# Eight of the 24 modulation groups computed between the prompt's attention maps, their weights loaded by Pool's queue

## The chip, the core and the metric

One core of one Trainium2 chip runs the whole program. The metric is the device time of one execution in microseconds (us). The kernel before took 1636.48 us (median of three runs). Engines are named as in the profile: PE (TensorE), DVE (VectorE), ACT (ScalarE), POOL (GpSimd) and SP (SyncE, which issues nearly all transfers; its queue of issues is SPq, Pool's is POOLq).

## The reference, cut to what matters

One layer of a streaming encoder, for a prompt of 512 rows and a running stream of 32 rows, width 1024, in float32:

```
mod = silu(c) @ w_ada + b_ada            -> shift1, scale1, gate1, shift2, scale2, gate2
h   = x * (1 + scale1) + shift1
z   = h @ w_in + b_in                    -> conv value, conv gate, q, k, v
conv: GLU -> causal depthwise conv (31 taps) -> LayerNorm -> swish
attention: rotary q/k, 4 heads, (softmax1 - lambda * softmax2) @ v, RMSNorm
x   = LN1(alpha * x + gate1 * (concat(conv, attn) @ w_out + b_out))
x   = LN2(alpha * x + gate2 * PEER(x * (1 + scale2) + shift2))
```

`w_ada` is 1024 by 6144, read once: 24 MB. Shift 1 and scale 1 are needed before anything else; gate 1 in the output projection; shift 2 and scale 2 after the first LayerNorm; gate 2 only at the very end.

## The kernel before, in words

The modulation is computed in 24 **groups** of 256 columns; group n belongs to vector n // 4 (shift 1, scale 1, gate 1, shift 2, scale 2, gate 2). `ada(n)` loads two tiles of 512 KB (r = 0 and 1), runs eight narrow float32 matmuls into a PSUM tile `pat` (L154), has ACT copy the result into `modrow` (L157), and queues the group in `PEND`. One group later `ada_end` closes it: for the four vectors in `cols` two tiny matmuls (L170) and a DVE write (L171); for groups from 8 on a load of the bias `bada` on SP (L176), a matmul with `sel4` (L178), a DVE add into `mrow` (L180) and a store to `mod_d` on SP (L181). PSUM tiles `sm` and `pat` come from two rings of two buffers each, which the attention uses too.

The stages, in program order:

1. Groups 0 to 7, the input x, and the first two column blocks of `w_in`.
2. Four channel blocks of the conv's value and gate (`zunit`, L194: one weight load, an ACT cast `wh` and a DVE rest `wl`, then 48 matmuls); after each block three groups, 8 to 19 in all. The GLU result goes to `U`; from then on the depthwise conv can run: 124 **taps** on DVE (L272, L275), one after the other on the accumulator `acc`, handed out by `conv(n)`.
3. The value columns (L322, L327, L333) in two halves, after each two groups, 20 to 23.
4. Keys and queries: `zqk(h)` for four heads. Each is two units of 48 matmuls (one for k, one for q), an ACT copy `z`, four transfers on SP that swap 32-row blocks into `zw` (L466), and three DVE operations (L468, L469, L471) which make the rotated `qk`; the key also goes out (L474).
5. Attention per head, four query blocks i: scores (L493), row maxima (L352), exponentials on ACT (L363), the difference map `a` (L383), transposes (L499), the product with v (L504), and `head_out`. Before head 2 come the rest of the taps and `conv_norm` (L401 to L418), before head 3 the sample's attention (L431 to L452).
6. The output projection (L607 to L631), LayerNorm, the PEER queries, and then the long pass over the two expert tables (to the end of the program).

What is written is not the order of execution: a scheduler orders each engine's instructions before the run, within the dependences and the rings. The taps are tied to each other by an order-only dependence. Transfers on SP leave in the order in which they stand in its queue, and an issue that waits holds back those behind it.

Weight tiles `wr` of all stages share a ring of eight buffers of 512 KB:

```
    def wload(src):
        t = wp.tile([128, D], F32, tag="wr", name="wr", bufs=WB)
        SY.dma_start(t, src)
        return t
```

Of the kernel before, what the change touches and what calls it, by code (L numbers as in the profile page):

```python
# [8 lines left out]
F32 = mybir.dt.float32  # L9
# [10 lines left out]
D = 1024  # L20
# [32 lines left out]
ROWB = 4  # L53
GSC = 2.0 ** 15
WB = 8
SLOT = 4.6
COST_U = 1.2
COST_V = 2.2
# [17 lines left out]
def build(tc, I, O):  # L76
# [3 lines left out]
    V, S, G, PE, SY = nc.vector, nc.scalar, nc.gpsimd, nc.tensor, nc.sync  # L80
# [12 lines left out]
    def pat():  # L93
        return pa.tile([128, 512], F32, tag="pa", name="pat")
# [24 lines left out]
    wp = pool(r1, "wp", 4, side="right")  # L119
# [13 lines left out]
# [4 lines that stand above are left out]
# [9 lines left out]
        V.tensor_sub(lo, t, hi.bitcast(F32))  # L146
        return hi, lo

    def ada(n, ps_=None):
        p = (ps_ or pat)()  # L150
        for r in range(2):
            w = wload(I["w_ada"][n, r])
            for g in range(4):
                PE.matmul(p[32 * g:32 * g + 32, :256], sil[:, r * 4 + g, :], w[:, g * 256:(g + 1) * 256],  # L154
                          start=(r == 0), stop=(r == 1), tile_position=(0, 32 * g))
        row = wp.tile([128, 256], F32, tag="modrow", name="modrow", bufs=3)
        S.copy(row, p[:, :256])  # L157
        PEND.append((n, row))
        if len(PEND) > 1:
            ada_end(*PEND.pop(0))  # L160

    PEND = []

    def ada_end(n, row):
        kind, q = divmod(n, 4)
        nm = ("sh1", "sc1", "g1", "sh2", "sc2", "g2")[kind]
        if nm in cols:
            c = sm()
            for s in range(2):
                PE.matmul(c[:, 2 * s:2 * s + 2], row[:, s * 128:(s + 1) * 128], sel4, start=True, stop=True)  # L170
            V.scalar_tensor_tensor(cols[nm][:, 2 * q:2 * q + 2, :], c[:, 0:4].rearrange("p (a b) -> p a b", b=2),  # L171
                                   float(nm[:2] == "sc"), bmod[nm][:, 2 * q:2 * q + 2, None].to_broadcast([128, 2, 2]),
                                   op0=OP.add, op1=OP.add)
        if kind >= 2:
            bt = wp.tile([2, 256], F32, tag="bada", name="bada", bufs=2)
            SY.dma_start(bt, bcast_rows(I["b_ada"][n * 256:(n + 1) * 256], 2))  # L176
            c = sm()
            PE.matmul(c[:2, :256], sel4, row, start=True, stop=True)  # L178
            rw = wp.tile([2, 256], F32, tag="mrow", name="mrow", bufs=1)
            V.tensor_add(rw, c[:2, :256], bt)  # L180
            SY.dma_start(mod_d[:, n * 256:(n + 1) * 256], rw)  # L181
# [47 lines left out]
    zp = pool(r5, "zp", 1, side="right")  # L229
# [18 lines left out]
    adas = iter(range(8, 24))  # L248
    for c in range(4):
        p1 = zbig(4 + c) if c else zfirst[0]  # L250
        sg = zp.tile([128, 2, HT], F32, tag="z", name="sg", bufs=2)
        S.activation(sg, p1[:, :, :HT], AF.Sigmoid, bias=bzc[:, 4 + c:5 + c])
        p0 = zbig(c) if c else zfirst[1]
        np2 = NP - HT
        for d0, h, s0, s1 in ((30, 0, 0, HT), (30 + HT, 1, 0, np2), (572, 1, np2, HT)):
            V.scalar_tensor_tensor(U[:, c, d0:d0 + s1 - s0], p0[:, h, s0:s1], bzc[:, c:c + 1], sg[:, h, s0:s1],
                                   op0=OP.add, op1=OP.mult)
        for n in range(3):
            ada(next(adas))
    SY.dma_start(O["convp"], U[:, :, 512:542])  # L260
    SY.dma_start(O["convs"], U[:, :, 574:604])
# [22 lines left out]
    def conv(n):  # L284
        for _ in range(n):
            next(taps, None)
# [25 lines left out]
    for n in range(2):  # L312
        wv = [wsplit(I["w_v"][n, kh]) for kh in range(2)]
        wf = WRAW[-2:]
        for i in range(NT):
            p = pat()
            r = ROWS[i]
            cs = [slice((k % 4) * 256, (k % 4 + 1) * 256) for k in range(KC)]
            if i < 4:
                for q, (a, b) in enumerate(((hh, 0), (hl, 0), (hh, 1))):  # L320
                    for k in range(KC):
                        PE.matmul(p[:, :256], a[:, k, i * 128:(i + 1) * 128], wv[k // 4][b][:, cs[k]],  # L322
                                  start=(q == 0 and k == 0), stop=(q == 2 and k == KC - 1))
            else:
                for k in range(KC):
                    o = k % 4 * 32
                    PE.matmul(p[o:o + 32, :256], hs[:, k, :], wf[k // 4][:, cs[k]], start=(k < 4), stop=(k >= 4),  # L327
                              tile_position=(0, o))
                vs4 = zp.tile([128, 256], F32, tag="vs4", name="vs4", bufs=1)
                S.copy(vs4, p[:, :256])  # L330
                p = sm()
                PE.matmul(p[:NS, :256], selrep[:, :NS], vs4, start=True, stop=True)
            V.tensor_add(vt[:r, i, n * 256:(n + 1) * 256], p[:r, :256], bv[:r, n * 256:(n + 1) * 256])  # L333
            if n == 1:
                SY.dma_start(O["v"][i * 128:i * 128 + r], vt[:r, i, :])
            conv(1)
        ada(next(adas))
        ada(next(adas))
    ada_end(*PEND.pop(0))
    S.activation(lsum, lsum, AF.Exp)  # L340
    V.tensor_sub(neglam, lsum[:, 1:2], lsum[:, 0:1])
    V.tensor_scalar(neglam, neglam, -LAM0, None, op0=OP.add)
# [137 lines left out]
    for h in range(4):  # L480
        if h < 3:
            qks.append(zqk(h + 1))
        qh, kh = qks[h]
        if h == 2:
            conv(124)
            conv_norm()
        if h == 3:
            sample_att()
        for i in ((0, 1, 2, 3) if h < 3 else (3, 0, 1, 2)):
            kl = 128 * (i + 1)  # L490
            sc = big()
            for m in range(2):
                PE.matmul(sc[:, m, :kl], qh[pT[m], i * 128:(i + 1) * 128], kh[pT[m], :kl], start=True, stop=True)  # L493
            V.memset(sc[:64, :, kl - 64:kl], NEG)
            e = at.tile([128, 2, 512], F32, tag="e", name="e")
            (a,), rs = softmax_parts([sc[:, :, :kl]], [e[:, :, :kl]], False)
            pt = sm()
            for kb in range(i + 1):
                PE.transpose(pt[:, kb * 128:(kb + 1) * 128], a[:, kb * 128:(kb + 1) * 128], ident)  # L499
            aT = at.tile([128, 512], F32, tag="aT", name="aT")  # L500
            (V.tensor_copy if h >= 3 else S.copy)(aT[:, :kl], pt[:, :kl])
            po = sm() if h < 3 else pat()
            for kb in range(i + 1):
                PE.matmul(po[:, :128], aT[:, kb * 128:(kb + 1) * 128], vt[:, kb, h * 128:(h + 1) * 128],  # L504
                          start=(kb == 0), stop=(kb == i))
            head_out(po[:, :128], i, h, 128, rs)
            conv(CB)
    r5.close()
    r4.close()
    l2 = ExitStack()  # L510
# [11 lines left out]
    for i in (4, 3, 0, 1, 2):  # L522
        r = ROWS[i]
# [574 lines left out]
    for q in range(2):  # L1098
        p = pat()
# [89 lines left out]
```

## Time and profile before

| what | before |
|---|---|
| three runs, us | 1636.06, 1636.48, 1637.83 |
| profiled execution, us | 1637.79 |
| its span, first to last instruction, us | 1635.8 |
| mean granted TensorE clock | 0.978 |
| PE busy | 1561.1 us (95%) |
| DVE busy | 1387.9 us (85%) |
| ACT busy | 611.2 us (37%) |
| POOL busy | 470.4 us (29%) |
| chain that ended last | PE 73%, DVE 13%, DMA 7% |

Busy time is the time in which an engine has an instruction under way; matmuls are pipelined, so a busy PE is not PE at its peak. The shares are averages over stages with different limits; stages 1 to 5 above fill the first 271 us, stage 6 the rest. A row of the timeline gives the start, the busy time, the engine, the line, output and inputs, the count, and in brackets the idle time ahead of it with what ended it.

### The profile page before, as it was taken

The page shows a single profiled execution, that of the slowest core. Times are in us where ns is not written, and L with a number is a line of the kernel's source. Part 1 is how long each engine was busy: PE and PEld are TensorE (multiplying, and loading weights), DVE is VectorE, ACT ScalarE, POOL GpSimd, SP SyncE. Part 2 cuts the span into 40 slices and gives each one's busy share as a digit, 9 for nine tenths or more (in the row PEclk, how much of TensorE's full clock was granted, in tenths as well). Part 3 has the DMA queues.
Part 4 walks back from the last instruction along what each step waited for, and adds up shares of the span by engine and source line. Part 5 has one row for each costly group of instructions (what it writes and reads, how often), then busy time and mean ns, then how long its engine had stood idle before and what let it go on. Part 6 is the DMA issues. An engine that isn't in the chain of part 4 may idle for free.

```text
span 1635.8 us, 24708 instructions
## 1 busy us (share of the span) xinstructions
PE 1561.1 (95%) x8887; PEld 1343.7 (82%) x8887; DVE 1387.9 (85%) x2680; ACT 611.2 (37%) x1059; POOL 470.4 (29%) x325
## 2 busy tenths in 40 slices
PE   7999987999989999999999899999999999999996
PEld 4777854786669999999999798888888888888884
DVE  3888988799999999999898568888778778788897
ACT  3312456342122444444454333333333333333332
POOL 0000000000144445247424123533334233244440
PEclk8999988999999999999999999999999999999998
DMA  9767333374478889999999999999999999999993
GB/s 348 282 193 258 87 117 122 97 225 141 157 242 283 293 279 314 342 351 337 365 350 376 354 311 313 345 358 342 349 338 342 340 329 352 337 321 329 336 327 104
DMA packets 184537, 465.58 MB, mean 285 GB/s; under 512 B 17536, under 2 KB 85184, under 8 KB 181216
## 3 DMA queue, kind: packets, MB, share of 16 engines
q1 hardware_dynamic: 138336, 296.23, 52.2%
q0 software_dynamic: 46080, 167.79, 29.1%
q8 instruction: 69, 1.13, 0.3%
q14 instruction: 52, 0.43, 0.1%
HBM read 415.57 MB, written 45.77 MB: 282 GB/s over the span
## 4 chain that ended last, share of the span: by engine, by line
PE 73%; DVE 13%; DMA 7%; issue 3%; ACT 2%; SPq 1%; DVEq 0%; POOL 0%; ACTq 0%; POOLq 0%
PE acc L1040 32%; PE pat L957 27%; PE big L194 3%; PE pat L731 2%; DMA rowg<-in_u_ji_dram,idx 2%; PE big L872 2%; PE big L620 1%; DVE jkg L904 1%; PE pat L154 1%; DVE acc L275 1%; DMA wr<-in_w_ada_dram 1%; DVE lo L948 1%; DVE s L710 1%; DMA wr<-in_w_in_dram 1%; DMA zw<-z 1%
## 5 line engine op out<-in xcount | busy, mean ns | idle before, releaser
L893 POOL DMA_INDIRECT rowg<-in_u_ji_dram,idx x160 | 210.9, 1318 | 790.5 <-DVE VT L707 438.4
L948 DVE TENSOR_TENSOR lo<-raw,hi 128x1024 fp32r<-128x1024 f32 x256 | 311.9, 1220 | 111.2 <-ACT hi L946 106.1
L946 ACT CAST hi<-raw 128x1024 fp32r<-128x1024 f32 x256 | 266.6, 1046 | 310.7 <-PE acc L1040 217.5
L893 POOL DMA_INDIRECT rowg<-in_vd_dram,idx x160 | 257.8, 1611 | 324.5 <-DVE accB L915 98.6
L1040 PE MATMUL acc<-hi,Pl 128*128 128x512 f32 x768 | 301.5, 393 | 0.0
L1040 PE MATMUL acc<-lo,Ph 128*128 128x512 f32 x768 | 281.4, 390 | 0.0
L1040 PE MATMUL acc<-hi,Ph 128*128 128x512 f32 x768 | 245.7, 394 | 3.7 <-issue 3.7
L957 PE MATMUL pat<-h2h,hi 128*128 128x384 f32 x1024 | 213.4, 343 | 5.9 <-ACT hi L946 2.8
L957 PE MATMUL pat<-h2h,lo 128*128 128x384 f32 x1024 | 210.6, 342 | 4.2 <-DVE lo L948 4.2
L957 PE MATMUL pat<-h2l,hi 128*128 128x384 f32 x1024 | 210.4, 341 | 0.0
L904 DVE SCALAR_TENSOR_TENSOR jkg<-rowg,xhB 128x1024 f16<-128x1024 f32 x160 | 195.0, 1218 | 12.0 <-DMA rowg<-in_u_ji_dram,idx 9.8
L915 DVE SCALAR_TENSOR_TENSOR accB<-rowg,wB,accB 128x1024 f32<-128x1024 f32 x158 | 201.8, 1277 | 0.5
L957 PEld LDWEIGHTS pat<-h2h,hi 128*128 128x128 f32 x1024 | 182.2, 189 | 13.1 <-ACT hi L946 5.4
L957 PEld LDWEIGHTS pat<-h2h,lo 128*128 128x128 f32 x1024 | 182.7, 189 | 7.9 <-DVE lo L948 4.8
L957 PEld LDWEIGHTS pat<-h2l,hi 128*128 128x128 f32 x1024 | 184.4, 189 | 2.6
L1040 PEld LDWEIGHTS acc<-hi,Ph 128*128 128x128 f32 x768 | 144.5, 189 | 31.3 <-issue 4.2
L1040 PEld LDWEIGHTS acc<-lo,Ph 128*128 128x128 f32 x768 | 144.4, 188 | 29.2
L1040 PEld LDWEIGHTS acc<-hi,Pl 128*128 128x128 f32 x768 | 145.0, 189 | 28.3
L963 ACT ACTIVATE ge<-pat 128x384 f32<-128x384 f32 x128 | 62.6, 491 | 195.0 <-PE pat L957 131.0
L1026 ACT CAST Ph<-P 128x384 fp32r<-128x384 f32 x128 | 65.1, 511 | 143.1 <-issue 89.9
L1028 DVE TENSOR_TENSOR Pl<-P,Ph 128x384 fp32r<-128x384 f32 x128 | 70.7, 553 | 33.2 <-ACT Ph L1026 32.9
L275 DVE SCALAR_TENSOR_TENSOR acc<-U,wdw,acc 128x574 f32<-128x574 f32 x120 | 96.6, 805 | 1.5
(320 smaller groups left out, 1853.7 us busy)
## 6 DMA issues: line engine op xcount, KB each, us to landing
raw<-in_uT_dram SPq DMA_DIRECT2D x128, 512.0 KB
raw<-in_vd_dram SPq DMA_DIRECT2D x128, 512.0 KB
wr<-in_w_ada_dram SPq DMA_DIRECT2D x48, 512.0 KB
g_d<-stg SPq DMA_DIRECT2D x24, 1024.0 KB
gc<-g_d SPq DMA_DIRECT2D x16, 1536.0 KB
wq<-in_w_query_dram SPq DMA_DIRECT2D x32, 512.0 KB
ge_d<-ge SPq DMA_DIRECT2D x70, 192.0 KB
gel<-ge_d SPq DMA_DIRECT2D x70, 192.0 KB
```

The source lines that it names most:

```text
L194: PE.matmul(p[h], a[:, k * 128:(k + 1) * 128], b[:, k, h * HT:(h + 1) * HT], start=(q == 0 and k == 0), stop=(q == 2 and k == KC - 1))
L275: t = V.scalar_tensor_tensor(acc[:, c], U[:, c, w:w + CO], wdw[:, c, w:w + 1], acc[:, c], op0=OP.mult, op1=OP.add)
L893: g = G.indirect_dma_start(out=t, out_offset=None, in_=tab, in_offset=bass.IndirectOffsetOnAxis(ap=idx, axis=0))
L904: V.scalar_tensor_tensor(jk, t, 1.0, h2B[s], op0=OP.mult, op1=OP.mult, accum_out=aB[s][:, q:q + 1])
L915: V.scalar_tensor_tensor(ac, t, w[:, q - c0:q - c0 + 1], ac, op0=OP.mult, op1=OP.add)
L946: S.copy(hi, raw)
L948: V.tensor_sub(lo, raw, hi.bitcast(F32))
L957: mm = PE.matmul(p[:, :NA], a[:, k * 128:(k + 1) * 128], b[:, k, :], start=(n == 0), stop=(n == 23))
L963: S.activation(ge, p[:, :NA], AF.Gelu)
L1026: S.copy(Ph, Pf)
L1028: V.tensor_sub(Pl, Pf, Ph.bitcast(F32))
L1040: mm = PE.matmul(accs[i][hf], a[:, sl], b[:, hs], start=(j == 0 and n == 0), stop=(j == NK - 1 and n == 2))
```

## The change

Three groups after each channel block become two (8 to 15), the four groups after the value columns go, and groups 16 to 23 are computed between attention maps: after the query blocks i < 3 of heads 0 and 1, and i < 2 of head 2. These eight load their weights by Pool's queue into a ring of their own, `wa`, with two buffers, that is one group's two tiles. The rings of `modrow` and `bada` shrink from 3 to 2 and from 2 to 1. The call that closed the last group ahead of the attention goes; what is pending is closed behind the last map.

```
+WAB = 2
...
-    def ada(n, ps_=None):
-        p = (ps_ or pat)()
+    def ada(n, side=False):
+        p = pat()
         for r in range(2):
-            w = wload(I["w_ada"][n, r])
+            if side:
+                w = zp.tile([128, D], F32, tag="wa", name="wa", bufs=WAB)
+                G.dma_start(w, I["w_ada"][n, r])
+            else:
+                w = wload(I["w_ada"][n, r])
...
-        row = wp.tile([128, 256], F32, tag="modrow", name="modrow", bufs=3)
+        row = wp.tile([128, 256], F32, tag="modrow", name="modrow", bufs=2)
...
-            bt = wp.tile([2, 256], F32, tag="bada", name="bada", bufs=2)
+            bt = wp.tile([2, 256], F32, tag="bada", name="bada", bufs=1)
...
-        for n in range(3):
+        for n in range(2):
             ada(next(adas))
...
             conv(1)
-        ada(next(adas))
-        ada(next(adas))
-    ada_end(*PEND.pop(0))
...
             conv(CB)
+            if i < (3, 3, 2, 0)[h]:
+                ada(next(adas), True)
+    while PEND:
+        ada_end(*PEND.pop(0))
```

The new order is seen at three places. Lines of the changed kernel are 5 higher than before from L154 on (the matmul L154 is L159, the store L181 is L186, the tap L275 is L280), and 2 higher in the attention (L466 is L468, L352 is L354, L493 is L495). An order row names the line, the operation, output and inputs, the shape of the output and how many follow each other.

On PE, where the first maps of head 0 are worked on. Before, matmuls of the next key and query units (L194) stand between the scores and the first transpose:

```order
L493 MATMUL big<-qk 128x384 x2
L493 MATMUL big<-qk 128x512 x2
L194 MATMUL pat<-hh,wh 128x272 x8
L194 MATMUL pat<-hh,wl 128x272 x7
L194 MATMUL pat<-hh,wh 128x272 x8
L194 MATMUL pat<-hh,wl 128x272 x9
L194 MATMUL pat<-hl,wh 128x272 x9
L499 MATMUL sm<-ident,a 128x128
```

Now, at the same place, stand groups 16 to 18 (`wa`) with the closings of the groups before them:

```order
L495 MATMUL big<-qk 128x512 x2
L159 MATMUL pat<-wa,sil 32x256 x8
L501 MATMUL sm<-ident,a 128x128
L506 MATMUL sm<-vt,aT 128x128
L175 MATMUL sm<-vec,modrow 128x2 x2
L183 MATMUL sm<-modrow,vec 2x256
L159 MATMUL pat<-wa,sil 32x256 x4
L501 MATMUL sm<-ident,a 128x128 x2
L506 MATMUL sm<-vt,aT 128x128 x2
L175 MATMUL sm<-vec,modrow 128x2 x2
L159 MATMUL pat<-wa,sil 32x256 x4
L495 MATMUL big<-qk 128x128 x2
```

The unit matmuls come later: of the eight key and query units, three stand ahead of the first score and five behind it, where it was four and four.

On SP, around the last two block swaps `zw` (key and query of head 3). Before:

```order
L474 DMA out_kT_dram<-qk 128x544
L466 DMA zw<-z 32x544 x7
L474 DMA out_kT_dram<-qk 128x544
L572 DMA rt<-in_b_out_dram 128x1024
L572 DMA rt<-mod_d 128x1024
L572 DMA row<-mod_d 128x1024
L466 DMA zw<-z 32x544 x4
```

Now the swap of the key stands behind three pairs of a store `mod_d` and a load `bada`, of which this is the last:

```order
L186 DMA mod_d<-mrow 2x256
L181 DMA bada<-in_b_ada_dram 2x256
L468 DMA zw<-z 32x544 x4
L476 DMA out_kT_dram<-qk 128x544
L578 DMA rt<-in_b_out_dram 128x1024
L578 DMA rt<-mod_d 128x1024
L468 DMA zw<-z 32x544 x4
```

Of the nine stores of `mod_d` still to come here (groups 15 to 23), three stand ahead of the key's swap of head 2 and three ahead of that of head 3; before, none stood behind the swaps of head 0.

On DVE, around the last tap. Before, only one map of head 2, the sample's attention and head 3 are left behind it:

```order
L352 TENSOR_REDUCE mx<-big 128x2
L376 SCALAR_TENSOR_TENSOR rl<-se,rc,neglam 128x1
L352 TENSOR_REDUCE mx<-big 128x2
L275 SCALAR_TENSOR_TENSOR acc<-U,wdw,acc 128x574
L383 SCALAR_TENSOR_TENSOR a<-e,rl 128x512
L357 TENSOR_TENSOR m_2611<-mx 128x2
L359 TENSOR_SCALAR nm<-m_2611 128x2
L404 TENSOR_TENSOR acc<-acc,pat 128x287 x4
```

Now both rotations of head 3 and two maps of head 2 are behind it as well:

```order
L185 TENSOR_TENSOR mrow<-sm,bada 2x256
L280 SCALAR_TENSOR_TENSOR acc<-U,wdw,acc 128x574 x4
L385 SCALAR_TENSOR_TENSOR a<-e,rl 128x256
L280 SCALAR_TENSOR_TENSOR acc<-U,wdw,acc 128x574
L470 TENSOR_TENSOR t_2212<-z,cosT 128x544
L471 TENSOR_TENSOR zw<-zw,sinT 128x544
L473 TENSOR_TENSOR qk<-t_2212,zw 128x544
L470 TENSOR_TENSOR t_2285<-z,cosT 128x544
L406 TENSOR_TENSOR acc<-acc,pat 128x287 x4
L496 MEMSET big 64x2x64
L354 TENSOR_REDUCE mx<-big 128x2
```

Of the 124 taps 91 stood ahead of the first row maximum before; now it is 73.

## Rows read from the trace of the kernel before

**Rows 1.** The page's head: span and instructions of the execution.

```profile
span 1635.8 us, 24708 instructions
```

**Rows 2.** Busy time by stretch: us, engines (instructions), granted PE clock, DMA share, GB/s.

```profile
core 0: us, PE busy (x) PEld busy (x) DVE busy (x) ACT busy (x) POOL busy (x), PEclk, DMA share, GB/s
0.00:52.20 52.20, 39.11 (x311) 24.09 (x311) 19.45 (x60) 20.34 (x37) 0.20 (x4) 0.87 0.95 359
52.20:103.90 51.70, 51.70 (x469) 44.22 (x469) 47.48 (x72) 12.08 (x19) 0.00 (x0) 1.00 0.62 231
103.90:143.50 39.60, 34.45 (x313) 27.64 (x312) 31.14 (x48) 8.04 (x12) 0.00 (x0) 1.00 0.73 221
143.50:174.90 31.40, 29.99 (x226) 27.68 (x226) 28.12 (x42) 8.05 (x16) 0.00 (x0) 1.00 0.61 205
174.90:232.20 57.30, 49.25 (x331) 37.59 (x330) 53.22 (x120) 28.39 (x103) 0.00 (x0) 0.90 0.38 116
232.20:271.20 39.00, 28.15 (x145) 18.20 (x147) 30.97 (x70) 28.07 (x80) 0.00 (x0) 0.81 0.16 57
271.20:330.00 58.80, 57.17 (x270) 41.42 (x262) 48.08 (x66) 24.57 (x41) 0.00 (x0) 0.99 0.39 131
330.00:1635.80 1305.80, 1271.31 (x6837) 1122.90 (x6837) 1129.39 (x2209) 481.62 (x755) 470.25 (x321) 0.99 0.88 309
```

**Rows 3.** Timeline of PE, 52 to 172 us: units, groups, closings, the first score.

```profile
52.18 2.26 PE L194 MATMUL big<-hh,wh 128*128 128x272 f32 x16 [0.35 <-ACT wh L144]
...
64.37 1.93 PE L154 MATMUL pat<-wr,sil 128*32 128x256 f32 x32
...
80.93 1.07 PE L154 MATMUL pat<-wr,sil 128*32 128x256 f32 x16
81.93 0.61 PE L170 MATMUL sm<-vec,modrow 128*128 128x2 f32 x4
...
89.96 0.59 PE L178 MATMUL sm<-modrow,vec 128*2 128x256 f32 x2
...
156.36 1.54 PE L194 MATMUL pat<-hl,wh 128*128 128x272 f32 x11
...
171.34 0.93 PE L493 MATMUL big<-qk 64*128 64x128 f32 x8
```

**Rows 4.** Timeline of DVE: first row maximum, a late swap, first weight rest of stage 6.

```profile
165.90 0.72 DVE L471 TENSOR_TENSOR qk<-t,zw 128x544 f32<-128x544 f32 x1
...
174.86 0.40 DVE L352 TENSOR_REDUCE mx<-big 128x2 f32<-128x256 f32 x1
...
218.76 0.72 DVE L469 TENSOR_TENSOR zw<-zw,sinT 128x544 f32<-128x544 f32 x1 [1.71 <-DMA zw<-z]
...
231.50 0.80 DVE L275 SCALAR_TENSOR_TENSOR acc<-U,wdw,acc 128x574 f32<-128x574 f32 x1
...
270.94 2.34 DVE L609 TENSOR_TENSOR wol<-wr,woh 128x1024 fp32r<-128x1024 f32 x2
```

**Rows 5.** The taps alone, 174.9 to 232.2 us: DVE busy (x), clock, DMA share, GB/s.

```profile
174.90:232.20 57.30, 25.25 (x33) 0.90 0.38 116
```

**Rows 6.** DVE by line, 49.4 to 271.2 us: busy us, mean ns, idle before.

```profile
L352 DVE TENSOR_REDUCE mx<-big 128x2 f32<-128x1024 f32 (+4 forms) x18 | 14.2, 794 | 0.0
L383 DVE SCALAR_TENSOR_TENSOR a<-e,rl 128x512 f32<-128x512 f32 (+3 forms) x17 | 9.0, 536 | 0.7 <-ACT e L380 0.7
L180 DVE TENSOR_TENSOR mrow<-sm,bada 2x256 f32<-2x256 f32 x15 | 6.1, 407 | 3.5 <-DMA mod_d<-mrow 3.5
L469 DVE TENSOR_TENSOR zw<-zw,sinT 128x544 f32<-128x544 f32 x8 | 5.8, 720 | 5.8 <-DMA zw<-z 5.8
```

**Rows 7.** SP's queue: its longest wait to 350 us, and the last swap issued.

```profile
SPq L181 <- DVE mrow L180: 31.3, 11, 7.9
...
210.00 2.73 SPq L466 DMA_DIRECT2D zw<-z  x4
```

**Rows 8.** ACT at the end of the attention: a table load ahead of the exponentials.

```profile
248.37 1.28 ACT L363 ACT_TABLE_LOAD   x1
```

**Rows 9.** Pool's gathers, 512 KB each: ns min/median/max, and us from issue to landing.

```profile
L893 POOL DMA_INDIRECT rowg<-in_u_ji_dram,idx x160: 932/1184/4489, 436.7 to 1535.5; - x160
...
DMA to landing us min/median/max: 4.3/7.4/11.7
```

## The prediction

> **What bounds the kernel now.** I read the busy time by stretch first, since a share over the whole span [rows 1] hides that the stages have different limits. The change touches the first 271 us; the long pass behind 330 us has PE busy 1271 of 1306 us and waits for what the early stages hand over, so it is taken to shift as a whole [rows 2]. Up to 52.2 us the transfers bound (DMA share 0.95). Then PE is busy all of 51.7 us, then 34.5 of 39.6, and up to the first row maximum 30.0 of 31.4. From there DVE bounds: 53.2 of 57.3 us until the last tap, while PE has 8 us of air. Behind the last tap nothing is full: DVE 31.0 of 39.0, PE 28.2 at a granted clock of 0.81 [rows 2]. So the kernel is PE-bound ahead of the attention and DVE-bound in it, with the 124 taps as the filler that keeps DVE full. Four marks carry the sum: first score 171.3 [rows 3], first row maximum 174.9, last tap done 232.2, first weight rest of the output projection 270.9 [rows 4].
>
> **The change part by part: ahead of the first score.** A unit of 48 matmuls takes 6.1 us (96 from 52.18 to 64.37), a group's eight matmuls 1.00 us (80.93 to 81.93), a closing matmul pair L170 or L178 about 0.55 us [rows 3]. By the new order PE has here 7 groups less than before in this stretch (the eighth one less stands ahead of 52.2 us), 12 closing pairs less and one unit less: 7.0 + 6.6 + 6.1 = 19.7 us. PE's 5.1 us of idle time in the value pass came with late weights; sixteen 512 KB loads leave SP's queue and so does the wait of SP for `mrow`, 31.3 us over eleven stores [rows 7], of which most stood in this stretch. I take half of the idle time, 2.5 us. First score: 171.3 - 19.7 - 2.5 = 149.1. It also needs the rotated query of head 0, which was done 8.7 us behind its unit (157.9 to 166.6) [rows 3, 4]: value pass over at 127.4, two units 12.2, then 8.7, which is 148.3; no new limit. DVE, less loaded now, follows 2.5 us later instead of 3.5: first maximum **151.6**.
>
> The first two `wa` loads fall due at about 45 us, when DMA is full: 1 MB at 359 GB/s is 2.9 us [rows 2]. The second pair of `w_in` tiles stands two loads earlier in SP's queue; I set the two against each other. The smaller rings cost nothing ahead of the attention: what hides them is that a closing stands a whole unit behind its group.
>
> **From the first maximum to the last tap.** Here DVE's work is counted, since it was the full engine. Only 73 taps are done instead of 91, so 18 more follow, at 0.765 us each (25.25 us for 33) [rows 5]: +13.8. Four row maxima move behind the last tap: -3.2 at 0.79; one map and the small operations of two: -1.2; one rotation (three operations of 0.72): -2.1; six `mrow` at 0.41: +2.4 [rows 6]. Sum +9.7: 62.9 us of work instead of 53.2. With 5 us of waits instead of 4 the last tap is over at **219.5**, 12.7 us earlier. PE's six groups, eleven closings and five units lie beside this; PE has, by the same prices and about 17 us for ten maps, 59 us to do in 68. That air is the cover; without it see the second rival.
>
> **Behind the last tap.** DVE has two rotations more (+4.3), four maxima (+3.2), one map and small ones (+1.2), three `mrow` (+1.2), two scalings of `otok` less (-1.2): 39.7 instead of 31.0 us [rows 2, 6]. And what is late next is the query of head 3. Its swap stands behind the key's, that behind three stores which each wait for an `mrow`, and behind two 512 KB rows for the projection. The same swap took 8.8 us from issue (210.0) to use (218.76), when taps covered all but 1.7 us [rows 4, 7]. Now: three operations 2.2, three issues 1.2, then 8.8, so 12.2 us behind the last tap, and DVE has some 7 us to do meanwhile: 5 us idle. The sample's attention waits for this, then the LayerNorm of the conv, and the four maps of head 3 come behind its swish on ACT, with a table load of 1.28 us between [rows 8]: some 3 us more, while about half of the old 8 us of waits go, since the norm no longer waits for maps. I take 10.5 us of waits: 50.2 us, mark **269.7** instead of 270.9. ACT's eight `modrow` copies only change place, and ACT is busy 28 of 57 us [rows 2].
>
> **Sum.** 12.7 us won up to the last tap, 11.5 given back behind it: -1.2 us. Against the profiled execution (1637.79 us, span 1635.8 and 2 around it) that is 1636.6; the median of the runs shown is 1.3 lower, so I say **1635.3 us**, no change that a measurement could tell: about 0.2%, 3.3 us, is what can be told from none.
>
> **Pool's loads**, which no row before shows directly: the nearest are the gathers of 512 KB, 0.93 us at least on POOL, 1.18 in the middle, and 4.3 to 11.7 us from issue to landing, in stretches with a DMA share of 0.88; here it is 0.38 [rows 2, 9]. I take the low end, 5.2 us per refill, because of that share; the far end is 12.9.
>
> The Trainium skill (SBUF - State Buffer, section "SBUF: two separate sides") speaks against this queue: a transfer issued by Pool has its descriptors written by Pool's cores, and these are locked out while DVE runs a copy in a two-port mode. In this trace half of the gathers were issued in 1.18 us or less, with DVE beside them, and the longest took 4.49 [rows 9]; the taps have two SBUF inputs and are no copies, so by rule and rows both the loads should go out. If the rule held for the taps too, the sum would be that of the third rival.
>
> **The rivals.**
> (a) *The head start is kept.* If the query's swap goes out early and the maps of head 3 fill the norm's gaps, DVE's waits behind the last tap are 4 instead of 10.5 us: -7.7, 1628.8 us. For it: SP's queue is short of large loads by then (DMA share 0.16 behind the last tap [rows 2]). Against: the order itself, which puts the swap behind stores.
> (b) *Refills hold PE up; slower.* Two buffers are one group, so groups 17, 18, 20, 21 and 23 wait for a refill that starts when the group before has been read. The order gives PE about 2.2 us of other work in between. At 5.2 us a round costs 3, at the median landing 6.1: 15 to 30 us in five rounds, against 9 us of PE's air. In part PE waits for DVE there anyway. Price: +6 us, 1641.3. It decides from about 2 us of visible wait per round.
> (c) *Pool is locked out.* At 4.49 us per issue instead of 0.93, two in a row, a round grows by 7 us; with half of it visible over five rounds +16, 1651.
>
> **How the numbers follow.** Forecast 0.47, (a) 0.28, (b) 0.19, (c) 0.03, and 0.03 for a worse order of the later stages, whose instructions the scheduler also moved. The forecast's own range is 1630.5 to 1639.5: each of the two waits, 5 and 10.5, may be off by 3 us. Of its 0.47, 0.09 lie more than 3.3 us below the median shown, 0.05 above; of (b) 0.03 stays within. Faster 0.28 + 0.09 = 0.37; same 0.33 + 0.03 = 0.36; slower 0.05 + 0.16 + 0.03 + 0.03 = 0.27. From 1627.5 to 1643 two in ten are left out: the good half of (a), (c), and the worst of (b).
>
> **What would show it.** First score near 149, last tap near 219 to 220, first weight rest at 268 to 272, and DVE idle ahead of the late swap by some 5 us: right. A gap of PE ahead of `wa` matmuls that ends with Pool's transfer, 2 us or more, five times: (b). Issues on POOL above 2 us: (c). A first weight rest before 265: (a), and the forecast is wrong; likewise if the last tap is not at least 8 us earlier, since then PE, not DVE, set the pace. Rows behind 330 us should be shifted alike; if not, the later order decided.

## The result and the profile after

The changed kernel took **1646.29 us** (median of five runs, 1645.55 to 1648.49) beside 1637.83 us for the kernel before in the same comparison: ratio 1.0057, 95% interval 1.0039 to 1.0075. It is slower; the forecast of 1635.3 us was wrong, and so was its range, which ended at 1643. The span of the profiled execution went from 1635.8 [rows 1] to 1644.8 us.

Busy time by stretch in the changed kernel, cut at the marks that answer to those of [rows 2]: start of the channel blocks, value pass, keys and queries, first row maximum, last tap, first weight rest, a late point, end. After the stretch come its length and busy us (count) of PE, PEld, DVE, ACT and POOL, then granted clock, DMA share and GB/s.

```profile
0.00:52.20 52.20, 40.20 (x296) 25.69 (x297) 18.53 (x58) 20.47 (x36) 1.48 (x6) 0.97 0.97 368
52.20:99.30 47.10, 47.10 (x399) 40.98 (x398) 40.62 (x59) 12.28 (x17) 0.00 (x0) 0.96 0.53 189
99.30:127.80 28.50, 27.46 (x235) 24.60 (x234) 25.59 (x41) 5.12 (x7) 0.00 (x0) 1.00 0.61 174
127.80:151.50 23.70, 22.02 (x171) 20.99 (x171) 21.26 (x29) 5.65 (x11) 0.00 (x0) 1.00 0.63 190
151.50:221.80 70.30, 61.05 (x414) 43.60 (x413) 63.45 (x134) 26.31 (x89) 6.35 (x12) 0.83 0.42 128
221.80:278.70 56.90, 44.01 (x265) 27.72 (x265) 39.86 (x90) 34.80 (x105) 1.05 (x2) 0.88 0.56 189
...
338.00:1644.00 1306.00, 1270.61 (x6837) 1122.43 (x6837) 1128.09 (x2209) 480.24 (x753) 471.80 (x321) 0.99 0.88 308
```

The four marks, from the changed kernel's timelines of PE and of DVE (start, us, engine, line, operation):

```profile
148.33 0.93 PE L495 MATMUL big<-qk 64*128 64x128 f32 x8 [0.77 <-DVE qk L473]
```

```profile
151.52 0.41 DVE L354 TENSOR_REDUCE mx<-big 128x2 f32<-128x256 f32 x1
...
221.09 0.81 DVE L280 SCALAR_TENSOR_TENSOR acc<-U,wdw,acc 128x574 f32<-128x574 f32 x1
...
278.67 1.20 DVE L615 TENSOR_TENSOR wol<-wr,woh 128x1024 fp32r<-128x1024 f32 x1
```

The first score comes 23.0 us earlier than before [rows 3], the last tap 10.4, and the first weight rest of the output projection 7.7 us **later** [rows 4]. The stretch between the last two grew from 38.7 to 56.9 us. The first matmul of the queries, behind all that the change touches, starts at 335.7 instead of 326.5, 9.2 later; from there to the end both take 1309 us.

A fifth mark turned out to say most: the end of PE's last key or query unit. It is at 208.2 us before and at **225.9** in the change, although PE starts the attention 23 us earlier. Here are the rows of PE for this mark, for its first matmul of the output projection and for the first of the queries, before:

```profile
207.57 0.62 PE L194 MATMUL pat<-hl,wh 128*128 128x272 f32 x3
...
267.22 1.22 PE L620 MATMUL big<-woh,mixh 128*128 128x512 f32 x2 [1.89 <-ACT woh L607]
...
326.46 2.34 PE L731 MATMUL pat<-h2fB,wq 128*128 128x160 f32 x16
```

and in the change:

```profile
224.77 1.17 PE L199 MATMUL pat<-hl,wh 128*128 128x272 f32 x8
...
278.57 0.73 PE L626 MATMUL big<-woh,mixh 128*128 128x512 f32 x2 [1.95 <-ACT woh L613]
...
335.66 2.34 PE L737 MATMUL pat<-h2fB,wq 128*128 128x160 f32 x16
```

### The profile page after: what moved, and what is told of

Its sections match the earlier page's. It is cut to its first block, busy times and chain, and to the rows that moved or that the text cites. A ratio compares the mean times of both kernels' runs of the same rounds, so it can differ in the third digit from the quotient of the medians.

```text
span 1644.8 us, 24693 instructions
## 1 busy us (share of the span) xinstructions
PE 1569.4 (95%) x8887; PEld 1348.1 (82%) x8887; DVE 1388.4 (84%) x2680; ACT 611.6 (37%) x1059; POOL 480.7 (29%) x341
## 4 chain that ended last, share of the span: by engine, by line
PE 70%; issue 12%; DVE 9%; DMA 6%; ACT 2%; SPq 0%; POOL 0%; DVEq 0%; ACTq 0%; POOLq 0%
PE acc L1046 32%; PE pat L963 30%; PE big L878 2%; DMA wa<-in_w_ada_dram 2%; DMA raw<-in_uT_dram 2%; PE pat L737 2%; PE big L626 1%; DMA rowg<-in_u_ji_dram,idx 1%; DVE s L716 1%; DVE jkg L910 1%; DVE IT L714 1%; DVE IT L718 1%; ACT hi L952 1%; DVE VT L713 1%; PE pat L159 1%
## 5 line engine op out<-in xcount | busy, mean ns | idle before, releaser
L910 DVE SCALAR_TENSOR_TENSOR jkg<-rowg,xhB 128x1024 f16<-128x1024 f32 x160 | 195.4, 1221 | 13.5 <-DMA rowg<-in_u_ji_dram,idx 10.5
L921 DVE SCALAR_TENSOR_TENSOR accB<-rowg,wB,accB 128x1024 f32<-128x1024 f32 x158 | 202.2, 1280 | 4.0 <-DMA rowg<-in_vd_dram,idx 3.5
L280 DVE SCALAR_TENSOR_TENSOR acc<-U,wdw,acc 128x574 f32<-128x574 f32 x120 | 96.5, 804 | 1.5
```

The lines of the kernel that those rows point to most:

```text
L280: t = V.scalar_tensor_tensor(acc[:, c], U[:, c, w:w + CO], wdw[:, c, w:w + 1], acc[:, c], op0=OP.mult, op1=OP.add)
L910: V.scalar_tensor_tensor(jk, t, 1.0, h2B[s], op0=OP.mult, op1=OP.mult, accum_out=aB[s][:, q:q + 1])
L921: V.scalar_tensor_tensor(ac, t, w[:, q - c0:q - c0 + 1], ac, op0=OP.mult, op1=OP.add)
```

## The experiments

Theories: **A**, head 3's swaps are late because of where they stand on SP's queue. **B**, refills of the two weight buffers hold PE up, so head 3's units are late. **C**, the two groups that stand behind the conv's norm lengthen the end. **D**, DVE sets the last tap, so PE's head start is worth little. All marks are us of the profiled executions; differences are taken before rounding. The kernel before took 1631 to 1646 us on the chips of these runs, and a ratio from medians and one profile's marks differ by up to some 4 us, in run 5 by 7. The last unit is the end of PE's last key or query unit, queries the first matmul of the PEER queries.

| kernel | first score | last unit | last tap | weight rest | queries | ratio to before, interval |
|---|---|---|---|---|---|---|
| before | 171.3 | 208.2 | 232.3 | 270.9 | 326.5 | |
| change | 148.3 | 225.9 | 221.9 | 278.7 | 335.7 | 1.0057, 1.0039 to 1.0075 |
| 1 swaps on ACT | 153.9 | 231.0 | 219.8 | 279.8 | 336.4 | 1.0078, 1.0053 to 1.0104 |
| 2 loaded once | 148.0 | 212.2 | 231.2 | 271.4 | 331.7 | 1.0034, 1.0017 to 1.0052 |
| 3 six groups | 158.5 | 233.0 | 218.9 | 281.9 | 340.9 | 1.0079, 1.0055 to 1.0103 |
| 4 SP, ring of 8 | 153.2 | 214.5 | 229.4 | 269.5 | 329.6 | 1.0016, 0.9998 to 1.0034 |
| 5 Pool, ring of 8 | 153.4 | 216.4 | 229.4 | 273.2 | 330.1 | 1.0066, 1.0044 to 1.0088 |
| 6 SP, 2 buffers | 146.9 | 221.2 | 224.8 | 277.1 | 332.3 | 1.0034, 1.0021 to 1.0047 |
| 7 groups left out | 151.8 | 187.7 | 226.2 | 258.1 | 316.0 | 0.9934, 0.9915 to 0.9953 |
| 8 as 4, rings of before | 153.0 | 207.7 | 232.0 | 269.6 | 329.9 | 1.0016, 1.0002 to 1.003 |
| 9 before, 106 taps | 169.2 | 205.7 | 201.8 | 265.3 | 320.5 | 0.9991, 0.9977 to 1.0005 |
| 10 change, 106 taps | 148.0 | 225.4 | 196.9 | 273.4 | 330.3 | 1.0025, 1.0011 to 1.0039 |
| 11 as 8, (2, 2, 2, 2) | 152.7 | 195.9 | 227.9 | 275.8 | 333.5 | 1.0048, 1.0028 to 1.0068 |
| 12 four groups | 156.8 | 202.2 | 229.2 | 262.2 | 320.0 | **0.9957**, 0.9941 to 0.9973 |
| 13 four, Pool, 2 buffers | 161.8 | 204.1 | 224.0 | 261.1 | 320.6 | **0.9958**, 0.9943 to 0.9973 |
| 14 four left out | 155.5 | 196.6 | 227.0 | 256.9 | 315.1 | 0.9949, 0.9932 to 0.9965 |
| 15 change, (2, 2, 2, 2) | 148.3 | 207.2 | 233.3 | 286.4 | 341.3 | 1.0117, 1.0095 to 1.0138 |

Since a scheduler orders the engines anew for every edit, each row also moves instructions: in runs 1, 3, 4, 5, 7, 8, 11 and 13 one unit more than in the change stands ahead of the first score, as in the kernel before.

**1. The swaps on ACT's queue.**

```diff
-                SY.dma_start(zw[32 * r:32 * r + 32], z[32 * (r ^ 1):32 * (r ^ 1) + 32])
+                S.dma_start(zw[32 * r:32 * r + 32], z[32 * (r ^ 1):32 * (r ^ 1) + 32])
```

> The change, with the four block swaps of each key and query issued on ACT's queue instead of SP's. Theory A (the swaps of head 3 are late, because they stand on SP's queue behind stores that wait and behind two 512 KB rows; in the change the query's swap takes 8 us from issue to its use on DVE): the DVE waits for the swaps of head 3 (1.45 and 2.84 us in the change) fall below 1 us, the stretch from the last tap to the first weight rest shrinks from 56.9 to some 50 to 52 us, time 1640 to 1642. Theory B (PE sets the pace in the attention: waits for the refilled weight buffers, each followed by some 10 us at half clock, make the units of head 3 late): last tap and tail within 2 us of the change, time 1645 to 1648; ACT may even lose 2 to 3 us by the issues.

Theory A falls. The rows from this run's timelines of ACT's queue and of DVE show why:

```profile
231.60 4.78 ACTq L468 DMA_DIRECT2D zw<-z  x4
```

```profile
242.16 0.72 DVE L471 TENSOR_TENSOR zw<-zw,sinT 128x544 f32<-128x544 f32 x1 [3.00 <-DMA zw<-z]
```

On a queue without stores and rows the query's swap was still used 10.6 us after its first issue (8.0 in the change). The unit itself was late (231.0), and PE had waited 8.3 us on `wa` by then.

What the late swaps have in common is the traffic beside them. The changed kernel's queue of SP around the two swaps of head 3 (key, then query):

```profile
219.99 2.41 SPq L468 DMA_DIRECT2D zw<-z  x4
...
226.94 2.41 SPq L468 DMA_DIRECT2D zw<-z  x4
229.39 0.58 SPq L578 DMA_DIRECT2D row<-mod_d  x1
230.01 3.84 SPq L596 DMA_DIRECT2D xp<-in_xtok_dram  x3
```

The key's swap was used 4.0 us after its first issue, at a DMA share of 0.29 from issue to use; in run 1 it was the same, 4.0 us at 0.29. The query's goes out as the projection's rows of 512 KB do (`rt`, `row`, `xp`): 8.0 us at 0.95 in the change, 10.6 at 1.02 in run 1, 8.8 at 0.93 before. That these rows hold the swap up is read from this, not tested: no run moved them.

**2. The weights loaded once.**

```diff
-                w = zp.tile([128, D], F32, tag="wa", name="wa", bufs=WAB)
-                G.dma_start(w, I["w_ada"][n, r])
+                if len(WA) < 2:
+                    WA.append(zp.tile([128, D], F32, tag="wa", name="wa", bufs=WAB))
+                    G.dma_start(WA[r], I["w_ada"][n, r])
+                w = WA[r]
```

> The change, but the two weight buffers of the moved groups are loaded once and used by all eight groups: it leaves out 14 of the 16 loads on Pool's queue, and computes seven groups from the wrong weights. Theory B (refills): no PE wait on wa (7.1 us in five in the change), granted clock above 0.95 instead of 0.83 between first maximum and last tap, the query unit of head 3 some 8 us earlier, tail 50 us or less, time 1637 to 1640. Theory A (swaps) or C (order of the norm, the sample's attention and the last two groups): gaps of 2 us close, but the tail stays above 54 us and the time above 1643.

Theory B holds for PE: with the same first score and the same five units behind it, the last unit is 13.8 us earlier, and the stretch behind the last tap is 40.2 instead of 56.9 us. At the queries 4.0 us of it are left, and the ratios (1.0034 and 1.0057) say 3.8; more was expected. From first score to last unit this run's window is:

```profile
148.00:212.20 64.20, 60.29 (x466) 47.42 (x468) 60.34 (x135) 29.85 (x99) 0.00 (x0) 0.97 0.18 50
```

PE idles 3.9 us at a clock of 0.97. The windows of the change over the same work:

```profile
148.30:160.00 11.70, 11.13 (x87) 8.49 (x87) 11.32 (x25) 6.84 (x19) 1.06 (x2) 1.00 0.40 111
160.00:178.00 18.00, 12.64 (x74) 7.15 (x74) 15.42 (x36) 5.59 (x22) 1.62 (x4) 0.62 0.56 181
178.00:196.00 18.00, 17.99 (x137) 14.84 (x135) 17.57 (x31) 6.02 (x21) 1.38 (x3) 1.00 0.26 70
196.00:214.00 18.00, 14.67 (x84) 8.72 (x84) 14.69 (x38) 7.14 (x28) 2.29 (x5) 0.72 0.58 173
214.00:225.90 11.90, 11.90 (x94) 11.34 (x94) 9.81 (x15) 3.29 (x11) 0.00 (x0) 1.00 0.14 41
```

PE idles 9.3 us of 77.6, and twice the clock falls. Here is what PE waited for at the first of the two places, and all its waits on `wa` from 148 to 226 us (us in total, times, longest):

```profile
160.53 0.59 PE L183 MATMUL sm<-modrow,vec 128*2 128x256 f32 x2 [0.47 <-ACT otok L393]
...
163.12 1.08 PE L159 MATMUL pat<-wa,sil 128*32 128x256 f32 x8 [1.99 <-DMA wa<-in_w_ada_dram]
...
166.13 0.69 PE L501 MATMUL sm<-ident,a 128*128 128x128 f32 x2 [1.92 <-DVE sh L176]
...
167.79 1.22 PE L506 MATMUL sm<-vt,aT 128*128 128x128 f32 x4 [0.98 <-ACT aT L503]
```

```profile
PE pat L159 <- DMA wa<-in_w_ada_dram: 2.9, 2, 2.0
```

Only 2.9 us of waiting on refills stand in the trace of that stretch. (The 7.1 us in five of the expectation add up the waits of PE's weight loads, 3.7, and of its matmuls, 3.4, in the whole program.) The rest of the 13.8 us is, as I read it, in what goes with it: while a group's second half waits, the maps' short matmuls and their waits on ACT and DVE are all that PE has, and in both places the clock falls to its lower level (1.2 of 2.4 GHz; 0.50 in 166 to 172 us), so what follows takes up to twice as long. How much of it lies in the order that the scheduler made for two slow buffers, and how much in the run itself, stays open.

**3. Six groups.**

```diff
             conv(1)
+        ada(next(adas))
...
-            if i < (3, 3, 2, 0)[h]:
+            if i < (3, 3, 0, 0)[h]:
```

> Six groups in the attention (three beside each of heads 0 and 1) instead of eight; the other two are computed in the value loop from the shared ring. Ahead of the first score PE has two groups and their closings more: first score at about 151 instead of 148.3. Theory C (the last two groups, which stand behind the norm's sums in PE's order with a wait for their refill and closings that hold up SP's queue, lengthen the tail): tail 52 us or less, time 1639 to 1642. Theory A or B: the tail stays above 55 us, the head start shrinks by 2 to 3 us, time 1645 to 1649.

A miss for theory C, and a lesson: the rest is at 281.9 with no group behind the norm at all. With the two groups one unit more went ahead of the first score (158.5, not 151), the six groups kept their rhythm, PE waited 4.3 us on `wa`, and the last unit came at 233.0. In runs 1, 3 and 10 the weight rest follows the last unit by 48 to 49 us, whatever else was changed; in the change by 52.7. So a unit that late seems to set the end.

**4 to 6. Queue and ring apart.** Run 4 loads through the shared ring on SP's queue:

```diff
-                w = zp.tile([128, D], F32, tag="wa", name="wa", bufs=WAB)
-                G.dma_start(w, I["w_ada"][n, r])
+                w = wload(I["w_ada"][n, r])
```

> The change, but the weights of the eight moved groups go through the shared ring of eight buffers on SP's queue, as before the change, not through two buffers on Pool's. If the two buffers or Pool's queue cost time (theory B), the waits on the weights go away and the time is 1638 to 1642. If SP's queue is the worse place (stores that wait for mrow hold the loads, and the loads hold the swaps), the time is 1647 to 1655. If neither matters: 1644 to 1648.

Run 5 keeps Pool's queue with the ring of eight, run 6 the two buffers with SP's queue:

```diff
+                w = wp.tile([128, D], F32, tag="wr", name="wr", bufs=WB)
+                G.dma_start(w, I["w_ada"][n, r])
```

> The loads of the moved groups stay on Pool's queue, but go into the shared ring of eight buffers instead of two of their own. Theory B1 (the two buffers are what costs, not the queue): no wait of PE on the weights of 1 us or more, the last key or query unit on PE ends at 212 to 216 us (225.9 in the change, 214.5 with SP's queue and the ring of eight), first weight rest 268 to 272, ratio to before 1.000 to 1.003. Theory B2 (Pool's queue costs): last unit at 222 or later, ratio 1.005 or more.

```diff
-                G.dma_start(w, I["w_ada"][n, r])
+                SY.dma_start(w, I["w_ada"][n, r])
```

> The other half of the pair: SP's queue, but the two buffers of the change. Theory B1: waits of PE on wa as in the change or longer, granted clock between first maximum and last tap below 0.88, last unit at 222 or later, first weight rest 276 or later, ratio 1.004 to 1.008. Theory B2: last unit 212 to 217, rest 268 to 272, ratio 1.000 to 1.003.

At the query matmuls, against before: two buffers +9.2 (Pool) and +5.8 (SP), eight +3.6 and +3.2. By these marks the two buffers cost 2.6 to 5.6 us, and with them Pool's queue 3.4 more. The ratios share it out otherwise: two buffers +9.3 (Pool) and +5.6 us (SP), eight +10.8 and +2.6. By them Pool's queue costs 4 to 8 us, and the two buffers 3.0 on SP's queue and nothing on Pool's, each good to some 4 us. The difference is run 5, whose profiled execution was the fastest of six (1640.27 us, median 1646.34), and whose ratio is what was expected if Pool's queue is to blame. So buffers and queue together, with the order that the scheduler makes around them, cost 6 to 7 us (the change against run 4); how much belongs to which is not settled.

**7. The eight groups left out** (no loads, matmuls or closings; scale 2 is one, gate 2 zero).

```diff
-            if i < (3, 3, 2, 0)[h]:
-                ada(next(adas), True)
...
+    zr = wp.tile([2, 256], F32, tag="mrow", name="mrow", bufs=1)
+    G.memset(zr, 0.0)
+    G.memset(cols["sc2"], 1.0)
+    for n in range(16, 24):
+        SY.dma_start(mod_d[:, n * 256:(n + 1) * 256], zr)
```

> Leaves out the eight moved groups altogether: their loads, matmuls, copies and closings; scale 2 is set to one and gate 2 to zero, and eight stores of zeros stand in for theirs. It is the upper bound of what any place for these groups can give. Theory D (DVE, not PE, sets the last tap: it is busy for some 179 us of the 230 before it in every kernel so far, and idle mostly ahead of the taps): the first score comes at 145 to 149, but the last tap only at 222 to 227, the tail stays at 36 to 40 us, and the time is 4 to 9 us under that of before (ratio 0.9945 to 0.9975). If PE's head start were worth its 20 us, the ratio would be 0.990 or less.

Removing them altogether is worth 10.5 us at the queries, not the 20 of PE's head start. The last tap moves by 6 us only: DVE has 179 us of work up to it here and before. Placed in the attention, the eight groups cost 13.6 us with run 4's loads (316.0 to 329.6) and 19.7 in the change, against 10.5 ahead of it. None of the loading schemes tried here makes this place pay for all eight.

**8. Longer rings for the closings** (modrow 3, bada 2, on run 4).

```diff
-        row = wp.tile([128, 256], F32, tag="modrow", name="modrow", bufs=2)
+        row = wp.tile([128, 256], F32, tag="modrow", name="modrow", bufs=3)
...
-            bt = wp.tile([2, 256], F32, tag="bada", name="bada", bufs=1)
+            bt = wp.tile([2, 256], F32, tag="bada", name="bada", bufs=2)
```

> The fourth run's kernel (SP's queue, shared ring of eight) with the closings' rings as before the change: three modrow and two bada buffers, for which there is room once the two wa buffers are gone. If the shorter rings cost time (mrow and bada turn around once per closing): last unit 2 us or more earlier than 214.5, ratio 0.998 to 1.000. If not: marks within 2 us of the fourth run's, ratio 1.000 to 1.003.

The last unit is 6.8 us earlier, the queries and the ratio are the same: the rings cost nothing that reaches the end.

**9 and 10. The last 18 taps left out**, before and in the change.

```diff
                 yield
+                if len(TAPS) == 106:
+                    return
```

> The kernel before, without the last 18 of the 124 taps (13.8 us of DVE; the last channel block's filter is cut short). Theory D (DVE is the full engine up to the last tap, and PE has air): the last tap comes 12 to 14 us earlier, at 218 to 220, the first weight rest 8 to 13 us earlier, at 258 to 263, ratio 0.992 to 0.995. If the maps' chain (PE, ACT and transfers) set the end already: rest at 267 or later, ratio 0.997 or more.

> The change, without the same 18 taps. Theory B (in the change PE, held up by refills and the low clock behind them, sets when head 3's keys and queries are ready, and with that the end): the last key or query unit stays at 222 to 227, the first weight rest moves by less than 4 us from 278.7, ratio to before 1.003 to 1.007. If DVE set the end in the change too: rest 10 us or more earlier, ratio 1.000 or less.

Before, 13.8 us of DVE work less bring 6.0 us at the queries (1.5 by the ratio, whose interval takes in no gain at all): theory D is half right at most, probably since the maps' chain follows closely behind. In the change the last unit does not move (225.4), and 5.2 us are won at the weight rest, probably since the norm is ready earlier. The bound of 4 us that B set was missed by 1.2.

**11. Two groups per head** (2, 2, 2, 2), on run 8.

```diff
-            if i < (3, 3, 2, 0)[h]:
+            if i < (2, 2, 2, 2)[h]:
```

> SP's queue, the shared ring of eight and the closings' rings of before, as in the eighth run, but two groups beside each of the four heads (2, 2, 2, 2) instead of (3, 3, 2, 0). Theory C (what is computed behind the norm lengthens the tail): tail 41 us or more (37.6 in the eighth run), ratio 1.002 to 1.005. If the groups fill PE's idle time there: last unit before 206, first weight rest 264 to 268, ratio 0.997 to 1.000.

Theory C holds in this form: with four groups behind the norm the last unit is the earliest of all kernels that do the whole work (195.9), and still the weight rest is 6.2 us later than in run 8. The late end of the change thus has two possible sources, late units and late groups; run 3 speaks for the first alone being enough.

**12. Four groups, one beside each head**, on run 8 (SP's queue, the longer rings), the other four in the channel blocks as before.

```diff
-        for n in range(2):
+        for n in range(3):
...
-            if i < (3, 3, 2, 0)[h]:
+            if i < (1, 1, 1, 1)[h]:
```

> Only four groups are moved (those of gate 2, which only the end of the program needs), one beside each head; the other four stay in the channel blocks, as before. SP's queue, the shared ring and the closings' rings of before. Leaving out all eight was worth 10.5 us up to the query matmuls, so four are worth some 5. If the attention absorbs one group per head: first weight rest 265 to 268, query matmuls 321 to 324 (326.5 before), ratio 0.997 to 0.999. If a group costs as much there as ahead of it: ratio 1.000 to 1.002.

This beats both kernels: 1630.46 us beside 1636.29 for the one before, more than was expected (0.997 to 0.999). From first score to last unit, and behind the last tap, its windows are:

```profile
156.80:202.20 45.40, 45.40 (x353) 38.72 (x353) 43.91 (x96) 21.50 (x71) 0.00 (x0) 1.00 0.37 113
229.20:262.20 33.00, 25.43 (x142) 16.08 (x142) 30.09 (x66) 23.07 (x66) 0.00 (x0) 0.79 0.30 98
```

PE does not idle once and keeps its full clock; behind the last tap DVE is busy 30.1 of 33.0 us.

**13 to 15. Is it the buffers or the rate?** Run 13 makes run 12's edit on the change itself, with its loads and rings; run 14 leaves run 12's four groups out, as run 7 did its eight; run 15 makes run 11's edit on the change.

> The twelfth run's four groups, one beside each head, but with the loads of the change: two buffers of their own on Pool's queue, and its shorter rings for the closings. Theory B (what costs is that a refill comes too late for the next group): with one group per head no wait on wa of 0.5 us or more, last unit within 3 us of the twelfth run's 202.2, first weight rest 262 to 266, ratio 0.995 to 0.998. If the two buffers or Pool's queue cost something by themselves (the scheduler's order around them, the queue): last unit 208 or later, rest 268 or later, ratio 1.000 or more.

> The twelfth run's kernel with its four moved groups left out altogether (gate 2 is zero, four stores of zeros stand in): the bound for any place for these four. If the attention absorbs one group per head: first weight rest and query matmuls within 2 us of the twelfth run's 262.2 and 320.0, ratio 0.994 to 0.997. If they cost there as much as ahead of it: 4 us or more earlier, ratio 0.991 to 0.994.

> The change with its eight groups placed two beside each head (2, 2, 2, 2) instead of (3, 3, 2, 0); loads and rings are the change's. Theory B: each refill has half a head's time, so the waits on wa before the last unit fall from 7 us to below 3 us and the last unit comes at 205 to 215 instead of 225.9; four groups in the tail cost what they cost in the eleventh run (first weight rest 275.8 there), so rest 275 to 281, ratio 1.004 to 1.007. If two buffers cost by themselves: last unit 222 or later.

Run 13 settles it for four groups: two buffers on Pool's queue, no wait on `wa` in its list of waits, the last unit at 204.1 and the same ratio as run 12. Neither the buffers nor Pool's queue cost anything there; they cost where several groups in a row want them. Run 14 says that the four groups cost 4.9 us in the attention by the marks (1.3 by the ratios), so which of its two expectations holds is open. Run 15 puts the last unit at 207.2 as theory B said, but its groups behind the norm wait for refills there too, 277.70 being the worst, right ahead of the projection:

```profile
277.70 0.64 PE L159 MATMUL pat<-wa,sil 128*32 128x256 f32 x8 [2.62 <-DMA wa<-in_w_ada_dram]
```

Its rest, 286.4, is 5 us later than the latest that was expected, and its ratio, 1.0117, lies above the range. Beside run 11, which has the same placement, the queries are 7.8 us later.

## Why the prediction was wrong, by its own steps

**Ahead of the first score: right.** 149.1 was forecast, 148.3 came; first maximum 151.6 and 151.5.

**Up to the last tap: right by its sum.** 62.9 us of DVE work and 5 of waits were forecast, 63.5 and 6.8 came, the last tap 2.4 us later than said. What failed here is the cover: "PE has, by the same prices and about 17 us for ten maps, 59 us to do in 68. That air is the cover". The prices were those of a PE at full clock that never waits. Between the same marks PE was busy 61.1 of 70.3 us, close to that sum, but at a clock of 0.83, and its units were not done. From the first score on it needed 68.3 us of busy time and 9.3 of waits to get through them, at a clock of 0.85, and ended 4 us behind the last tap.

**Behind the last tap: the step that failed, "I take 10.5 us of waits".** DVE's work was right (39.9 us, 39.7 forecast); its waits were 17.0. Part of the miss is in the sum: 5 us for the swap, 3 for norm and maps and the half of the old 8 that stays come to 12, not 10.5. The other 5 were not foreseen. The longest waits, from the changed kernel's list of DVE's waits from 221.9 to 278.7 us:

```profile
DVE zw L471 <- DMA zw<-z: 4.3, 2, 2.8
DVE mx L354 <- PE big L435: 4.2, 1, 4.2
DVE rc L373 <- ACT e L365: 3.2, 2, 1.6
DVE crs L417 <- ACT crs L416: 1.4, 1, 1.4
```

The query's swap cost 2.8 us (the key's 1.5), and 5 were forecast; the query's rotation came 13.1 us behind the last tap, and 12.2 were forecast. What was missed is that this wait is passed on. The timelines of DVE, ACT and PE show how:

```profile
223.98 0.72 DVE L471 TENSOR_TENSOR zw<-zw,sinT 128x544 f32<-128x544 f32 x1 [1.45 <-DMA zw<-z]
...
230.84 1.23 DVE L354 TENSOR_REDUCE mx<-big 128x2 f32<-128x1024 f32 x1
...
234.91 0.72 DVE L471 TENSOR_TENSOR zw<-zw,sinT 128x544 f32<-128x544 f32 x1 [2.84 <-DMA zw<-z]
...
235.63 0.15 DVE L361 TENSOR_SCALAR nm<-mx 128x2 f32<-128x2 f32 x1
...
244.08 1.35 DVE L354 TENSOR_REDUCE mx<-big 128x2 f32<-128x1024 f32 x2 [4.20 <-PE big L435]
```

```profile
235.81 0.69 ACT L365 ACTIVATE e<-big,nm 128x512 f32<-128x512 f32 x1 [3.00 <-DVE nm L361]
```

```profile
237.31 0.35 PE L435 MATMUL big<-ks,qs 64*32 64x32 f32 x12 [3.38 <-ACT e L365]
237.88 4.19 PE L412 MATMUL pat<-csq,ones_c 128*128 128x287 f32 x8 [0.22 <-ACT csq L410]
242.00 1.93 PE L433 MATMUL big<-wr,qs 64*32 64x512 f32 x4
...
244.51 2.10 PE L412 MATMUL pat<-csq,ones_c 128*128 128x287 f32 x8
```

The scaled maximum `nm` of head 2's last map stands behind the rotation in DVE's order, and waits for the swap with it, though its input was there at 232.07. ACT's exponentials wait for `nm`, the sample's scores on PE for the `big` tile that those read, and behind them stand eight sums of the norm, at half clock 4.19 us (the next eight took 2.10 at full clock). Only then come the last scores, and DVE waits again. The transfer was late once; four waits on three engines were the price.

**Rival (b) came nearest, but its price fits by luck.** Refills were given +6 us. At the queries run 4, with other buffers and another queue, is 6.0 us better than the change, and the pair of medians, 1.0057 and 1.0016, says 6.7; run 2, which leaves out 14 of the 16 loads, is 4.0 better. But the price came from gaps that are not there: of "a gap of PE ahead of `wa` matmuls ... 2 us or more, five times" the trace has one of 2.0 us, and two below 1. A refill was also quicker than the 5.2 us assumed; from the chain of waits of the change, issue to landing (PE waited for the first two, not for the others):

```profile
158.48 4.60 DMA wa<-in_w_ada_dram
...
195.12 4.80 DMA wa<-in_w_ada_dram
...
201.38 3.76 DMA wa<-in_w_ada_dram
...
208.54 3.88 DMA wa<-in_w_ada_dram
```

The cost was in late units and the clock, not in the gaps. Even so (b) gave 1641.3 in all, 5 us too low. The rest of the miss is the place itself: with run 4's loads the eight groups still make the queries 3.2 us later than before (2.6 by the ratio), where the forecast had them 1.2 earlier.

The weight rest hides this. In run 4 it is where it was forecast (269.5 and 269.7), but 60.1 us pass from there to the queries instead of 55.6. The rows of PE shown above say why: before, PE began the projection 3.7 us ahead of the weight rest (267.2), in the change 0.1 ahead (278.6), in run 4 level with it (269.6). So by PE's own start the change is 11.4 us late, not 7.7, and run 4 2.3 late, not 1.4 early. From that start to the queries PE has some 265 matmuls in each: 59.2 us before, at a clock of 0.96, 57.1 in the change at 1.00, and 60.1 in run 4 at 0.95. The projection was taken as a plain shift of the weight rest, and it is not.

**The rest.** Rival (a) fell with the late units. Rival (c) fell too (its price, half of 7 us in five rounds, comes to 17.5 and not 16): Pool issued its 16 loads in 0.53 us each, 0.72 at most, with DVE busy 68.8 of 77.6 us:

```profile
L155 POOL DMA_DIRECT2D wa<-in_w_ada_dram x16: 530/530/719, 44.2 to 248.2; - x16
```

On the rule that was weighed in the prediction (the Trainium skill, SBUF - State Buffer, "SBUF: two separate sides"): the taps beside these issues are no copies, and no issue was held up, so the trace agrees with it as read there. That the smaller rings cost nothing that reaches the end (run 8), and that the stages behind the queries only shift (1309 us in both), was right.

## What to carry to other kernels

Air on an engine is a cover only while the engine keeps its clock and its order: price the moved work at the clock of the stretch that it will make, and ask which late product (here head 3's query unit) sets the end, not how full the engines are. Work with a slow refill goes where the time between two uses is longer than the refill; one group per head hid it with two buffers, three beside each of two heads did not. And before moving work, leave it out once: that gives about the most that any place for it can bring (here 10.5 us at the queries for eight groups; moving four won 6.5). The bound is a rough one, since the order changes with it: leaving out four alone gave 11.4 (run 14). And a mark on one engine, such as the weight rest, is not the start of the stage on another.

## What was not expected of the hardware

A 512 KB load on Pool's queue landed in 3.8 to 4.8 us, at the low end of the gathers (4.3 to 11.7) [rows 9]: 4.6 and 4.8 at a DMA share of 0.8, 3.8 and 3.9 at 0.4 to 0.6. A swap (four issues of 68 KB) was used 4.0 us after the first of them at a DMA share of 0.29, and 8.0 to 10.6 us after it at 0.93 to 1.02. On ACT's queue an issue of it took 0.60 us in the middle, on SP's 0.59. And short waits were dear on PE: with 5.4 us of idle time between 160 and 168 us it ran at half clock (0.50 in 166 to 172, still 0.70 in 172 to 178), with some 3 us between 196 and 200 it did again (0.50 in 202 to 208), while run 12, with no wait at all in 45.4 us, kept the full clock.
